# Instruction costs, diagonal scores and state order in a one-core decoder layer

## The chip, the core and the metric

One Trainium2 chip, one of its cores. The metric is the device time of one execution in microseconds (us): 1038.59 us is the median of three runs of the kernel before (1036.82 to 1039.56). A core has four compute engines that run side by side, each through its own queue in order: TensorE (PE) multiplies matrices, VectorE (DVE) and GpSimd (POOL) work elementwise, ScalarE (ACT) evaluates functions and casts. SyncE (SP) issues the large loads. An instruction starts when it is first in its queue and the semaphores that it waits for are there.

## The reference: one layer of a hybrid decoder

512 tokens of width 1024 pass through a mixing stage, a cross attention into 256 memory tokens, and a mixture of experts (32 experts). The change lies in the mixing stage. One input projection of the normalised tokens gives the columns of two branches and of their gates; the branches are projected back and merged:

```python
def conformer_conv_branch(a, gate, w_dw, b_dw, ln_g, ln_b, w_proj):
    u = a * jax.nn.sigmoid(gate)
    u = causal_depthwise_conv(u, w_dw, b_dw)          # 31 taps
    u = jax.nn.silu(layer_norm(u, ln_g, ln_b))
    return u @ w_proj
...
    def step(state, inp):                             # HGRN2, per chunk and head
        qb, kb, vb, fb = inp
        cum = jnp.cumsum(fb, axis=2)
        o_inter = jnp.einsum('bhtk,bhkv->bhtv', qb * jnp.exp(cum), state)
        ...
        scores = jnp.einsum('bhtk,bhtsk,bhsk->bhts', qb, decay, kb)
        o = o_inter + jnp.einsum('bhts,bhsv->bhtv', scores, vb)
        ...
```

Here `f` is the log of the forget gate, `k = 1 - f`, four heads of 128. The output of the recurrence is normalised per head, multiplied by `silu(g)` and projected by `hgrn_w_out`; the convolution's by `conv_w_out`. Each is multiplied by a sigmoid gate per channel (two gates of 1024 channels), the sum goes through `w_mix_out`.

## The kernel before: threads between the matmuls of the projections

**The projections.** `gemm_t` runs a projection with its output transposed (channels on partitions): 256 output columns at a time in two PSUM banks (`pt`), the contraction in chunks of 4 x 128. Inputs and weights are split into a high and a low part of type fp32r, and each product takes three matmuls of 128x512 (`hh` or `hl` by `wh` or `wl`); a chunk has 24 of them. A chunk's weights go a fixed way: SP loads `raw` (two buffers at this place), ACT casts it to `wh`, POOL subtracts to get `wl` in two pieces, TensorE multiplies. `ahead()` issues the splits three chunks ahead. The projections follow one another: V, f, q, u (the convolution's input, in four parts), g, the two gates (16 columns of 128, `ev_gate`), then `ev_rec` (from `oh`/`ol`, the recurrence's output split) and `ev_conv` (from `ch`/`cl`, the convolution's).

**The threads.** Between two matmul groups `pump()` steps generators: `hgrn_scores` (ending in `hgrn_state`), started before the q projection, and `conv`, started before u. A generator yields a time, and `pump` resumes it when the clock of the work issued has come to it. The clocks are kept by `Meter`: one for each of DVE, ACT, POOL and PE, which adds an estimated cost for every instruction at build time and holds the time at which each tile is ready. So the cost functions `dve_cost`, `act_cost`, `pool_cost` and `pe_cost` set the order of the program; on the chip the order is fixed.

**The recurrence.** `hgrn_scores` takes logarithms of `cum` (f) and `ck` (k) on ACT, four head pairs, then running sums along the tokens on DVE (`tensor_tensor_scan`, printed as SCALAR_TENSOR_TENSOR in the program order), and `ck = cum - ck`. Then for each of seven levels (blocks of 64, 32, ... 1 tokens) it makes a tile `z` (two subtractions on DVE, exp on ACT, one product with q on DVE), from which TensorE makes the scores of that level (`psc`), written into `ST` on ACT or DVE. The diagonal scores, `scores(7, kT, qT, ...)`, need only k and q: 16 matmuls in four banks, and four masked copies on DVE. `hgrn_state` goes through the four token blocks: outputs `po`, state updates `pst`, then a normalisation, and for each head four transposes of `oN` on TensorE (`pot`), a product into `gT` on DVE and the split `oh`/`ol`.

**The convolution.** 31 taps on DVE, for two channels blocks at a time, into PSUM banks (`cva`), reading `uT`. Then a layer norm over channels: column sums by eight matmuls of ones (`pmu`, and after the squares `pvar`), the root on DVE (`rsqrt_steps`), and for each of four blocks scaling on DVE, tanh on ACT, a product, and the split `ch`/`cl`.

**The buffers.** Tiles of 128x2048 (`unit`, `u4`) come from a ring of 16 buffers in the order in which the program asks for them; who asks gets the oldest buffer and waits until its last reader is done. Four gate tiles of four columns each are asked for in `ev_gate`, each at its first column.

Weights and threads aside, the experts' weights are loaded by SP from about 490 us on, and the stage behind 560 us is limited by these loads.

Of the kernel before, what the change touches and what calls it, by code (L numbers as in the profile page):

```python
# [42 lines left out]
class Meter:  # L43

    ready, port = {}, []

    def __init__(self, engine, cost):
        self.engine, self.cost, self.clock = engine, cost, 0.0  # L50
# [1 line left out]
    def __getattr__(self, name):  # L52
        f = getattr(self.engine, name)

        def call(*args, **kw):
            out = args[0] if args else kw["out"]
            aps = [a for a in list(args) + list(kw.values()) if hasattr(a, "tensor")]
            t = max([self.clock] + [Meter.ready.get(a.name, 0) for a in aps if a is not out])
            c = self.cost(out, kw)
            if name == "tensor_tensor" and c > 300 and all(a.space == SB for a in aps):  # L60

                for t0, t1, e in Meter.port[-4:]:
                    if e is not self and t0 <= t < t1:
                        t = t1
                Meter.port.append((t, t + c, self))
            self.clock = t + c
            for a in (out, kw.get("accum_out")):
                if a is not None:
                    Meter.ready[a.name] = self.clock + 60
            return f(*args, **kw)  # L70

        return call
# [28 lines left out]
def tile_layer(ctx, tc, x, mem, norm_mix_g, w_in, conv_w, conv_b, conv_ln_g, conv_ln_b, conv_w_out,  # L101
# [4 lines left out]
    nc = tc.nc  # L106
    meters = [Meter(e, c) for e, c in ((nc.vector, dve_cost), (nc.scalar, act_cost), (nc.gpsimd, pool_cost),
                                       (nc.tensor, pe_cost))]
    Meter.ready, Meter.port = {}, []
    V, S, G, PE = meters  # L110

    def dump(name, ap):
# [24 lines left out]
    def q4(name, dt=F32, tag="o"):  # L137
        return pool.tile([128, 1024], dt, name=name, tag=tag, bufs=BUFS[tag])

    def bank(name):  # L140
        return psum.tile([128, 512], F32, name=name, tag="b")
# [69 lines left out]
    done = set()  # L211

    def now():

        return max(m.clock for m in meters[:2])
# [409 lines left out]
    def hgrn_state():  # L625
        ST, qe, ke, elast = (state[n] for n in ("ST", "qe", "ke", "elast"))
        hs = q4("hs")[:, :512].rearrange("p (h v) -> p h v", h=4)
        oN = u4("oN")
        ssq, y, t = st[:, 16:32], st[:, 32:48], st[:, 48:64]
        sq = q4("sq")  # L630
        for b in range(NB):
            po = bank("po")
            for h in range(NH):
                sl = slice(h * 128, (h + 1) * 128)
                PE.matmul(po[:, sl], lhsT=ST[:, b, sl], rhs=Vn[b][:, sl], start=True, stop=b == 0)
                if b:
                    PE.matmul(po[:, sl], lhsT=qe[:, h, b * 128:(b + 1) * 128], rhs=hs[:, h, :],
                              start=False, stop=True)
            if b < NB - 1:
                pk = bank("pk")  # L640
                for h in range(NH):
                    PE.transpose(pk[:, h * 128:(h + 1) * 128], ke[:, h, b * 128:(b + 1) * 128], ident)
                kn = q4("kn")[:, :512]
                S.copy(out=kn, in_=pk)
                yield S.clock + 1500
                pst = bank("pst")
                for h in range(NH):
                    sl = slice(h * 128, (h + 1) * 128)
                    PE.matmul(pst[:, sl], lhsT=kn[:, sl], rhs=Vn[b][:, sl], start=True, stop=True)
                if b == 0:  # L650
                    S.copy(out=hs, in_=pst.rearrange("p (h v) -> p h v", h=4))
                else:
                    for h in range(NH):
                        V.scalar_tensor_tensor(hs[:, h, :], hs[:, h, :], elast[:, h * 4 + b:h * 4 + b + 1],
                                               pst[:, h * 128:(h + 1) * 128], op0=OP.mult, op1=OP.add)
            yield meters[3].clock + 1000
            S.copy(out=oN[:, b, :], in_=po)
            yield
            for h in range(NH):
                S.activation(sq[:, :128], oN[:, b, h * 128:(h + 1) * 128], AF.Square,  # L660
                             accum_out=ssq[:, b * 4 + h:b * 4 + h + 1])
            yield now()

        rsqrt(ssq, y, t, 4 * 128)
        V.tensor_scalar(y, y, 0.5, None, op0=OP.mult)
        for b in range(NB):
            ov = oN[:, b, :].rearrange("p (h v) -> p h v", h=4)
            V.tensor_tensor(out=ov, in0=ov, in1=y[:, b * 4:b * 4 + 4, None].to_broadcast([128, 4, 128]), op=OP.mult)
            yield
        yield now()  # L670
        yield from until("g")
        ohl.extend((u4("oh", F32R), u4("ol", F32R)))
        for h in range(NH):
            ps = bank("pot")
            for b in range(NB):
                PE.transpose(ps[:, b * 128:(b + 1) * 128], oN[:, b, h * 128:(h + 1) * 128], ident)
            V.scalar_tensor_tensor(gT[:, h, :], ps, vec("on", 0), gT[:, h, :], op0=OP.mult, op1=OP.mult)
            yield V.clock
            S.activation(ohl[0][:, h, :], gT[:, h, :], AF.Copy, scale=0.5)
            V.scalar_tensor_tensor(ohl[1][:, h, :], gT[:, h, :], 0.5, ohl[0][:, h, :].bitcast(F32),  # L680
                                   op0=OP.mult, op1=OP.subtract)
            yield V.clock

    def hgrn_scores():
# [62 lines left out]
        for li, m in enumerate(LEVELS):  # L747
            z = u4("z")
            zv, cv, qv, kv = (t.rearrange("p c (n two m) -> p (c n) two m", two=2, m=m) for t in (z, cum, qT, ck))
            mid = cv[:, :, 0, m - 1:m].to_broadcast([128, 1024 // m, m])  # L750
            V.tensor_tensor(out=zv[:, :, 0, :], in0=mid, in1=kv[:, :, 0, :], op=OP.subtract)
            V.tensor_tensor(out=zv[:, :, 1, :], in0=cv[:, :, 1, :], in1=mid, op=OP.subtract)
            yield V.clock
            S.activation(z, z, AF.Exp)
            ez = S.clock
            yield
            if prev is None:
                yield from until("q")
            else:
                yield from top_scores(prev, 2 * m, at) if li < 3 else scores(li - 1, prev, prev, at)  # L760
            yield ez
            V.tensor_tensor(out=zv[:, :, 1, :], in0=zv[:, :, 1, :], in1=qv[:, :, 1, :], op=OP.mult)
            at = V.clock + 2500
            yield
            prev = z
        yield from scores(7, kT, qT, 0)

        qe, ke = u4("qe"), u4("ke")
        state["qe"], state["ke"] = qe, ke
# [29 lines left out]
    def conv():  # L799
# [9 lines left out]
        for c2 in (0, 2):  # L809
# [12 lines left out]
            if c2 == 0:  # L822
                cv = u4("cv")
                chl.extend((u4("ch", F32R), u4("cl", F32R)))
            yield V.clock
            for c in (c2, c2 + 1):
                split(acc[c], c)
                S.copy(out=cv[:, c, :], in_=acc[c])
# [58 lines left out]
    def ev_gate(i, ps):  # L887
        w, i = i // 8, i % 8
        if i % 4 == 0:
            gates[w][i // 4] = u4("gate")  # L890
        S.activation(gates[w][i // 4][:, i % 4, :], ps, AF.Tanh, scale=0.5)

# [988 lines left out]
```

## Time and profile before

| | |
|---|---|
| median of three runs | 1038.59 us (1036.82 to 1039.56) |
| the profiled execution, its own time | 1040.21 us |
| its span in the profile | 1038.5 us |
| TensorE busy | 965.6 us, 93% |
| DVE, ACT, POOL busy | 479.6, 284.2, 255.5 us |
| mean granted clock of TensorE | 0.968 |

The profile gives one execution. The span is cut into stretches by the windows view: for each engine the busy time and the count of instructions, then the granted clock as a share of full speed. A timeline row is an instruction, or a run of the same, with its start and duration; the brackets give the idle time of the engine just ahead of it and what released it. The chain of waits is followed back from the last instruction of a stretch, and each piece is what the next one waited for. Matmuls are pipelined: one of 128x512 shows 0.39 us, but a row of them follows at a closer distance. All recorded instructions have line L70 before and L76 after, which is the line of the helper that records them.

### The profile page before, as it was taken

The numbers are of one execution on the slowest core, as the hardware profiler recorded it, in microseconds if no ns is written. First come the engines' busy times: TensorE is split into PE (matmuls) and PEld (weight loads), VectorE is DVE, ScalarE is ACT, GpSimd is POOL, SyncE is SP. The second block draws the span as 40 slices with busy tenths as digits, with TensorE's granted clock in tenths as the row PEclk, the third lists the DMA queues.
The fourth block names the chain that finished last, engine by engine and source line by source line (L and its number), as shares of the span: only waits on it lengthen the run. The fifth ranks groups of instructions, "written<-read, shape, count | busy, mean of one in ns | idle before, by whom it ended". The sixth has DMA issues, their size and how long they took to land.

```text
span 1038.5 us, 13293 instructions
## 1 busy us (share of the span) xinstructions
PE 965.6 (93%) x4951; PEld 630.0 (61%) x4951; DVE 479.6 (46%) x967; ACT 284.2 (27%) x467; POOL 255.5 (25%) x201
## 2 busy tenths in 40 slices
PE   7999989999999999999999999999879999687774
PEld 6888878888888788988874444444325544122221
DVE  6670567897976742545235233333203553010103
ACT  5633552335434333354411111011001110000003
POOL 2364642423445596341310000000000000000001
PEclk9999989999999999999999999999989999887988
DMA  9433221222323232224877999999999999999993
GB/s 339 170 88 102 82 64 58 62 82 68 96 63 100 89 116 88 73 83 171 344 282 293 382 373 418 417 418 415 420 417 419 418 418 416 419 418 419 415 391 139
DMA packets 80671, 260.81 MB, mean 251 GB/s; under 512 B 8475, under 2 KB 39356, under 8 KB 59996
## 3 DMA queue, kind: packets, MB, share of 16 engines
q1 hardware_dynamic: 75194, 252.81, 63.2%
q0 software_dynamic: 1728, 3.80, 1.0%
q10 hardware_dynamic: 3682, 3.32, 0.9%
q8 instruction: 40, 0.66, 0.3%
q14 instruction: 27, 0.22, 0.1%
HBM read 258.21 MB, written 4.19 MB: 253 GB/s over the span
## 4 chain that ended last, share of the span: by engine, by line
PE 69%; DMA 21%; DVE 5%; ACT 2%; SPq 2%; issue 1%; ACTq 0%; DVEq 0%
PE pt L70 24%; PE pg L70 12%; PE pn L70 12%; DMA wg<-in_moe_w_gate_dram 7%; DMA wd<-in_moe_w_down_dram 6%; PE py L70 5%; DMA wu<-in_moe_w_up_dram 5%; PE psc L70 3%; PE pc L70 3%; DMA raw<-in_xa_w_v_dram 2%; PE pd L70 2%; DVE z L70 1%; PE pot L70 1%; PE px L70 1%; PE pw L70 1%; DVE cum L70 1%
## 5 line engine op out<-in xcount | busy, mean ns | idle before, releaser
L70 POOL TENSOR_TENSOR wl<-raw,wh 128x512 fp32r<-128x512 f32 x158 | 219.1, 1409 | 288.3 <-ACT wh L70 288.0
L70 PE MATMUL py<-wd,sghd 128*32 128x512 f32 (+2 forms) x512 | 115.5, 645 | 18.8 <-DMA wd<-in_moe_w_down_dram 18.6
L70 ACT CAST wh<-raw 128x1024 fp32r<-128x1024 f32 x88 | 92.0, 1050 | 125.8 <-PE pt L70 75.3
L70 PE MATMUL pg<-wg,XT 128*32 128x512 f32 (+2 forms) x512 | 106.3, 624 | 12.4 <-DMA wg<-in_moe_w_gate_dram 12.2
L70 PE MATMUL pt<-hh,wh 128*128 128x512 f32 x288 | 115.0, 399 | 0.0
L70 PE MATMUL pt<-hh,wl 128*128 128x512 f32 x288 | 113.0, 392 | 0.0
L70 PE MATMUL pt<-hl,wh 128*128 128x512 f32 x288 | 112.9, 392 | 0.0
L70 PE MATMUL pg<-wu,XT 128*32 128x512 f32 (+2 forms) x512 | 104.8, 633 | 6.7 <-DMA wu<-in_moe_w_up_dram 6.6
L70 DVE TENSOR_TENSOR xs<-pc,xs 128x512 f32<-128x512 f32 x96 | 58.5, 680 | 89.4 <-PE pc L70 89.4
L70 POOL DMA_INDIRECT X<-xd,idx x12 | 12.1, 1008 | 343.9 <-DVE idx L70 174.8
L70 PEld LDWEIGHTS py<-wd,sghd 128*32 128x32 f32 (+2 forms) x512 | 31.8, 133 | 93.6 <-issue 54.4
L70 DVE SCALAR_TENSOR_TENSOR yl<-py,wsl,yh 128x512 fp32r<-128x512 f32 x26 | 19.4, 750 | 135.6 <-ACT yh L70 134.3
L70 PEld LDWEIGHTS pg<-wg,XT 128*32 128x32 f32 (+2 forms) x512 | 31.5, 132 | 82.7 <-issue 58.8
L70 DVE SCALAR_TENSOR_TENSOR cva<-uT,ca,cva 128x482 f32<-128x482 f32 (+29 forms) x120 | 78.6, 730 | 0.0
L70 PEld LDWEIGHTS pg<-wu,XT 128*32 128x32 f32 (+2 forms) x512 | 30.7, 132 | 73.1 <-issue 54.8
L70 PEld LDWEIGHTS pt<-hh,wl 128*128 128x128 f32 x288 | 54.5, 189 | 11.7
L70 PEld LDWEIGHTS pt<-hl,wh 128*128 128x128 f32 x288 | 54.7, 190 | 10.9
L70 PEld LDWEIGHTS pt<-hh,wh 128*128 128x128 f32 x288 | 54.7, 190 | 10.9
L70 ACT COPY sghd<-ph 128x512 f32<-128x512 f32 x13 | 7.6, 586 | 159.1 <-PE ph L70 159.1
L70 ACT ACTIVATE yh<-py,wsl 128x512 fp32r<-128x512 f32 x26 | 17.9, 688 | 116.8 <-PE py L70 116.5
L70 DVE SCALAR_TENSOR_TENSOR sghd<-pg,wsl,sghd 128x512 f32<-128x512 f32 x13 | 9.8, 751 | 84.3 <-PE pg L70 71.4
L70 PE MATMUL pt<-h,wh 128*128 128x512 f32 (+1 forms) x160 | 41.4, 348 | 0.0
(324 smaller groups left out, 1560.4 us busy)
## 6 DMA issues: line engine op xcount, KB each, us to landing
wg<-in_moe_w_gate_dram SPq DMA_DIRECT2D x57, 1024.0 KB
wd<-in_moe_w_down_dram SPq DMA_DIRECT2D x56, 1024.0 KB
wu<-in_moe_w_up_dram SPq DMA_DIRECT2D x52, 1024.0 KB
raw<-in_w_in_dram SPq DMA_DIRECT2D x40, 512.0 KB
wu<-in_moe_w_up_dram SPq DMA_DIRECT2D x24, 512.0 KB
wd<-in_moe_w_down_dram SPq DMA_DIRECT2D x16, 512.0 KB
wg<-in_moe_w_gate_dram SPq DMA_DIRECT2D x14, 512.0 KB
raw<-in_xa_w_v_dram SPq DMA_DIRECT2D x4, 1024.0 KB
```

The lines of the kernel that those rows point to most:

```text
L70: return f(*args, **kw)
```

## The change: costs of scans and table loads, order of diagonal, state and gate

The costs: a `tensor_tensor_scan` counts 1.75 times its former cost, and an activation that changes between Ln and any other function counts 1300 ns more on ACT's clock. In `hgrn_state` each block's output waits in the thread for a time `th` set from when the state tile is ready, and the thread marks `"st"` as done behind its loop over blocks. The diagonal scores move from behind the levels to the first level, right behind q. The convolution's split of its sums is stepped 1000 ns later. In `ev_gate`, a gate tile other than the first is asked for only when the recurrence's thread has been stepped through to `"st"`.

```diff
-    ready, port = {}, []
+    ready, port, log = {}, [], [False]
...
             c = self.cost(out, kw)
+            if name == "tensor_tensor_scan":
+                c *= 1.75
+            if name == "activation" and (args[2] == AF.Ln) != Meter.log[0]:
+
+                Meter.log[0] = not Meter.log[0]
+                c += 1300
...
-    Meter.ready, Meter.port = {}, []
+    Meter.ready, Meter.port, Meter.log = {}, [], [False]
...
         sq = q4("sq")
+        th = 0
         for b in range(NB):
+            yield th
             po = bank("po")
...
                                                pst[:, h * 128:(h + 1) * 128], op0=OP.mult, op1=OP.add)
+                th = Meter.ready[hs.name] + 500
             yield meters[3].clock + 1000
...
             yield now()
+        done.add("st")
...
             if prev is None:
                 yield from until("q")
+                yield from scores(7, kT, qT, V.clock + 1500)
             else:
...
             prev = z
-        yield from scores(7, kT, qT, 0)
...
                 chl.extend((u4("ch", F32R), u4("cl", F32R)))
-            yield V.clock
+            yield V.clock + 1000
...
         if i % 4 == 0:
+
+            while i + w and "st" not in done:
+                step(t_sc)
             gates[w][i // 4] = u4("gate")
```

The order of SP and of POOL stays as it was; that of ACT, DVE and TensorE differs between the f projection and the one from `ch`/`cl`. On TensorE, 216 split matmuls of the q projection and of u stand ahead of the first scores before (the first level's 16, then 21 split matmuls and the next level); after, 222 stand ahead of the diagonal's 16, and 24 more between these and the first level. Three other places are shown.

ACT, at the logarithms (`cum` and `ck` from f and k; `qT` is the q projection's tanh, `wh` the weight cast), before:

```order
L70 ACTIVATE cum<-cum 128x512
L70 ACTIVATE ck<-kT,tiny 128x512
L70 CAST wh<-raw 128x1024
L70 ACTIVATE cum<-cum 128x512
L70 ACTIVATE ck<-kT,tiny 128x512
L70 ACT_TABLE_LOAD
L70 ACTIVATE qT<-pt 128x512 x2
L70 CAST wh<-raw 128x1024 x2
```

and after:

```order
L76 ACTIVATE cum<-cum 128x512
L76 ACTIVATE ck<-kT,tiny 128x512
L76 ACT_TABLE_LOAD
L76 ACTIVATE qT<-pt 128x512
L76 ACT_TABLE_LOAD
L76 ACTIVATE cum<-cum 128x512
L76 ACTIVATE ck<-kT,tiny 128x512
L76 ACT_TABLE_LOAD
L76 ACTIVATE qT<-pt 128x512
L76 CAST wh<-raw 128x1024 x2
```

The first q column has moved in front of the last pair of logarithms, and there are two table loads more.

ACT, at the first column of the third gate tile (`gate`; buffer numbers tell the tiles apart: 2382 before and 2378 after are that tile, `oh` is the recurrence's output, `ch` and `cv` the convolution's), before:

```order
L70 ACTIVATE oh_2290<-gT_1671 128x512 [waits DVE_49]
L70 ACTIVATE gate_2382<-pt_2312 128x512 [waits DVE_49,PE_49]
L70 ACTIVATE gate_2382<-pt_2313 128x512 [waits PE_49]
L70 CAST wh_2413<-raw_2366 128x1024 [waits DMAHW2_49,Activation_49,Pool_49]
L70 ACTIVATE oh_2290<-gT_1671 128x512
L70 CAST wh_2450<-raw_2418 128x1024 [waits PE_49,DMAHW3_49,Activation_49,Pool_49]
L70 ACTIVATE gate_2382<-pt_2411 128x512 [waits PE_49]
L70 CAST ch_2001<-cva_2015 128x512
```

and after:

```order
L76 ACTIVATE gate_2378<-pt_2310 128x512 [waits PE_49]
L76 ACTIVATE gate_2378<-pt_2311 128x512
L76 CAST wh_2403<-raw_2362 128x1024 [waits DMAHW2_49,Activation_49,Pool_49]
L76 CAST wh_2444<-raw_2408 128x1024 [waits DMAHW3_49,Activation_49,Pool_49]
L76 ACTIVATE oh_2272<-gT_1667 128x512 [waits DVE_49]
L76 ACTIVATE gate_2378<-pt_2401 128x512
L76 ACTIVATE gate_2378<-pt_2402 128x512 [waits PE_49]
L76 CAST wh_2491<-raw_2449 128x1024 [waits DMAHW4_49,Activation_49,Pool_49]
L76 ACTIVATE oh_2272<-gT_1667 128x512 [waits DVE_49]
L76 CAST ch_2026<-cva_2055 128x512
```

The first eviction waited for DVE (the convolution's reads of `uT`) and TensorE before; after, it has the buffer of `oN`, and TensorE's transposes are what it waits for. One more `wh` cast stands ahead of `ch`.

TensorE, behind the column sums of the squares (`pvar`; `hh`, `hl` are the normalised tokens of the gate projection, `oh`, `ol` the recurrence's output of the next projection), before:

```order
L70 MATMUL pvar<-ch,onesr 128x512
L70 MATMUL pvar<-cl,onesr 128x512
L70 MATMUL pt<-hh,wh 128x512
L70 MATMUL pt<-hl,wh 128x512
L70 MATMUL pt<-hh,wl 128x512
```

and after:

```order
L76 MATMUL pt<-hh,wl 128x512
L76 MATMUL pt<-oh,wh 128x512
L76 MATMUL pt<-ol,wh 128x512
L76 MATMUL pt<-oh,wl 128x512
L76 MATMUL pvar<-ch,onesr 128x512
L76 MATMUL pvar<-cl,onesr 128x512
```

Before, 18 matmuls of the gate projection and 96 of the projection from `oh`/`ol` follow `pvar` up to the first that reads `ch`; after, 93 of the latter.

## Rows read from the trace of the kernel before

**Rows 1.** Busy time of each engine by stretch: us, instructions, granted clock, DMA share, GB/s

```profile
100.00:165.00 65.00, 60.65 (x346) 51.03 (x345) 35.86 (x29) 32.02 (x36) 31.18 (x19) 0.92 0.24 73
165.00:305.00 140.00, 140.00 (x745) 120.13 (x745) 121.98 (x184) 50.18 (x88) 49.94 (x38) 1.00 0.24 72
305.00:360.00 55.00, 54.04 (x237) 43.67 (x235) 38.45 (x49) 25.66 (x38) 30.07 (x22) 1.00 0.31 96
```

**Rows 2.** What TensorE waits for, 95 to 365 us: total us, times, longest

```profile
PE psc L70 <- DVE z L70: 4.4, 3, 2.2
```

**Rows 3.** Timeline of TensorE, 130 to 166 us: start, duration, what, count [idle before <- releaser]

```profile
135.31 2.05 PE L70 MATMUL psc<-z 128*64 128x64 f32 x32 [1.66 <-DVE z L70]
...
149.41 6.66 PE L70 MATMUL psc<-z 128*128 128x64 f32 x32 [2.17 <-DVE z L70]
...
156.82 0.63 PE L70 MATMUL pt<-hh,wl 128*128 128x512 f32 x1
157.25 0.63 PE L70 MATMUL pt<-hh,wh 128*128 128x512 f32 x1
```

**Rows 4.** Chain of waits, 100 to 215 us, in order of time: start, us, what

```profile
127.97 2.79 DVE z L70 x2
...
163.56 3.52 PE psc L70 x32
...
193.43 0.89 PE psc L70 x8
```

**Rows 5.** Busy time by stretch as in rows 1, one short stretch

```profile
150.00:160.00 10.00, 10.00 (x39) 9.13 (x39) 6.26 (x7) 2.61 (x2) 3.21 (x2) 0.50 0.20 60
```

**Rows 6.** Timeline of ACT, 104 to 147 us

```profile
114.22 0.71 ACT L70 ACTIVATE ck<-kT,tiny 128x512 f32<-128x512 f32 x1
114.95 1.28 ACT L70 ACT_TABLE_LOAD   x1
116.24 0.60 ACT L70 ACTIVATE qT<-pt 128x512 f32<-128x512 f32 x1
```

**Rows 7.** Timeline of DVE, 114 to 150 us

```profile
117.48 6.67 DVE L70 TENSOR_TENSOR_SCAN cum<-ca,cum 128x512 f32<-128x512 bf16 x4
```

**Rows 8.** Timeline of ACT, 286 to 330 us

```profile
302.31 1.09 ACT L70 ACTIVATE gate<-pt 128x512 f32<-128x512 f32 x2 [11.26 <-DVE cva L70]
...
312.70 1.05 ACT L70 CAST wh<-raw 128x1024 fp32r<-128x1024 f32 x1 [1.72 <-DMA raw<-in_w_in_dram]
...
326.37 1.05 ACT L70 CAST wh<-raw 128x1024 fp32r<-128x1024 f32 x1 [2.44 <-DMA raw<-in_hgrn_w_out_dram]
```

**Rows 9.** Chain of waits, 300 to 362 us

```profile
305.02 0.44 PE pot L70 x4
...
310.78 15.67 PE pt L70 x69
326.44 1.86 PE pvar L70 x8
...
357.36 0.70 DVE cl L70
...
358.10 3.93 PE pt L70 x16
```

**Rows 10.** Timeline of POOL, 284 to 330 us

```profile
304.41 5.50 POOL L70 TENSOR_TENSOR wl<-raw,wh 128x512 fp32r<-128x512 f32 x4 [11.26 <-ACT wh L70]
...
319.73 6.10 POOL L70 TENSOR_TENSOR wl<-raw,wh 128x512 fp32r<-128x512 f32 x4 [2.90 <-ACT wh L70]
```

**Rows 11.** Timeline of DVE, 326 to 362 us

```profile
344.83 1.37 DVE L70 TENSOR_TENSOR cl<-cv,ch 128x512 fp32r<-128x512 f32 x1 [0.68 <-ACT ch L70]
...
351.49 0.69 DVE L70 SCALAR_TENSOR_TENSOR gate<-gate,pt 128x512 f32<-128x512 f32 x1 [1.21 <-PE pt L70]
```

**Rows 12.** Timeline of TensorE, 766 to 778 us, in the expert stage

```profile
768.90 1.04 PE L70 MATMUL py<-wd,sghd 128*32 128x512 f32 x2 [2.22 <-DMA wd<-in_moe_w_down_dram]
```

**Rows 13.** Busy time by stretch as in rows 1, in the expert stage

```profile
771.00:778.00 7.00, 6.00 (x22) 1.15 (x26) 0.00 (x0) 0.00 (x0) 0.00 (x0) 0.51 1.02 414
```

## The prediction, made before the changed kernel ran

> **What bounds the kernel now.** I began with the busy time by stage [rows 1]. In 165:305 TensorE is busy without a break; in 100:165 it lacks 4.35 us of 65 and its granted clock is 0.92; in 305:360 it lacks 0.96 us. So in the part that the change touches TensorE sets the time, and time can be won only where it waits or runs slowly. The program order shows the same instructions on every engine from the w_mix projection (about 362 us) on; what is won or lost before 362 us therefore reaches the expert stage unchanged, where the loads follow the frees of TensorE's buffers. I take it one to one to the end.
>
> The second view is what TensorE waits for in 95:365: nearly everything is psc on DVE's z, 4.4 us in three waits, the longest 2.2 [rows 2]. The timeline of TensorE [rows 3] puts them at 135.3 (1.66 us) and 149.4 (2.17 us), with a short one between; the reader is to see that the score matmuls at 149.41 take 6.66 us, whereas the same 32 take 3.52 us at 163.56 [rows 4], and that the split matmuls behind them stand 0.43 us apart [rows 3] instead of the 0.227 that I work out below. The granted clock of 150:160 is 0.50 [rows 5]: right after the third wait TensorE drops to the lower level, 1.2 GHz, for 10 us.
>
> **Early part: what goes.** The waits for z come from a late chain on ACT and DVE. With the diagonal scores moved ahead, TensorE has 16 score matmuls and 24 split matmuls in front of the first level. Walk of the new order: ACT's last logarithm ended at 114.93 [rows 6]; without the fourth pair (about 1.2 us) it comes to the load at 113.7. Then load (1.28), qT (0.60), load, the fourth pair, load, qT: 120.0. DVE multiplies that qT (0.7) and starts its four scans at 120.7 instead of 117.48 [rows 7]; ck, the third q column and the two halves of z stand behind them as before and end 3.2 us later, the second half at 134.0 instead of 127.97 + 2.79 = 130.8 [rows 4]. The last q column (0.6) is there at 134.6. TensorE has done 222 split matmuls instead of 216 by then: before, the 216 ended at 133.5 (135.31 less the wait of 1.66, [rows 3], rounded for the tail of a matmul), so 6 more end at 134.9. The diagonal's four banks take 4 x 0.89 [rows 4] to 138.4. DVE's copies and z times q end near 140.5. TensorE's 24 split matmuls end at 143.85, so the first level has 3.3 us of cover; the following levels have, by the same count, 2.3, 1.2 and 4.0 us. The narrow place is the diagonal itself, with 0.3 us. I cost it at nothing; if it is missed it costs what it is missed by.
>
> Gain: the three waits, 4.4 us [rows 2], and the lower clock: 6.66 - 3.52 = 3.1 for the scores and nine split matmuls at 0.43 - 0.227, 1.8. Together **-9.3 us**. Ends: -4.4 if a new wait makes the clock fall once more there, -9.3 if none does.
>
> **The two additional table loads** lie in that walk at 1.28 us each. Before, the load starts 0.02 us after the last logarithm ends, and qT starts 0.01 us after the load ends [rows 6], so a switch costs its load and nothing around it.
> The Trainium skill, "ScalarE: Activation LUTs", section "What ACT_TABLE_LOAD costs", adds a pipeline drain of about 1.4 us to a load of about 1.3. By that the two extra switches would come to 5.3 us, an estimate from that page, and the sum would be 2.5 us worse at the diagonal; the rows of this trace show the load and not the drain.
>
> **Middle: the gate tile behind the state.** Before, ACT stood 11.26 us at the first column of the third gate tile for the convolution, whose input tile had the buffer [rows 8]. Now that tile takes the buffer of oN, which the fourth group of head transposes reads last. In the new order TensorE has 54 split matmuls (0.227 each: 15.67 us for 69) and two groups of transposes (0.44 each, [rows 9]) between that column's last matmul and the end of that group: 13.1 us in which ACT stands, with two gate evictions, two wh casts and the rest queued behind it, POOL's wl behind the casts, and raw's loads on SP behind wl. The weights split ahead last for 60 split matmuls, so 6 (1.4 us) are left when ACT is released. ACT then needs 0.6 + 0.5 + 1.05 (gates x2 and wh, [rows 8]) = 2.1: TensorE waits 0.8. The first wl comes 1.4 us later [rows 10], two matmuls (0.45) cover part: 0.9 more. Then the loads: before, the next wh but one came 10.4 us after ACT's release because its raw had just landed [rows 8]; the convolution's ch and cl were cast in front of it, now they stand behind it. raw can be loaded when wl has read the buffer, 4.9 us after release, and lands 3.6 to 5.5 us after that: a wh waits for it until 326.37 and 312.70 [rows 8], and the first half of POOL's four wl ahead of each ended at 322.8 and 307.2 [rows 10]. With 3.6: wh ends at 9.6 us after release, then oh 0.6 and two rounds of ch, cl, cv at about 1.9, that is 14 us less what pmu's first matmuls can do while the last halves are made (some 1.9): about 12 against the 9.9 (36 x 0.227 + 1.7) at which TensorE comes to pmu. I take 2.3, **+4.0 us** for the middle. Bounds: 0 if the casts are as little in the way as before, when the stall of 11.26 us cost TensorE nothing, and 6 with the landing of 5.5.
>
> **Tail: the variance.** From the end of pvar to the last cl there is a chain on DVE and ACT: 326.44 + 1.86 to 357.36 + 0.70 is 29.8 us [rows 9], of it 0.68 idle in DVE ahead of each of two cl and 1.21 ahead of a gate [rows 11]. TensorE has 114 split matmuls behind pvar before the first that reads ch, and ten more to the first that needs the last cl: 124 x 0.227 = 28.1, so 1.6 us are late; they stand as waits and a broken pipeline just ahead of 358.10 [rows 9]. In the new order pvar stands 21 split matmuls later: 93 + 10 = 103, 23.4 us. Two of the gate multiplications come into the reciprocal root and fewer stand between the last casts, so the chain is between 27.2 (no idle) and 29.8; I take 28.5. Late by 5.1 instead of 1.6: **+3.5 us** (1.9 to 4.8).
>
> **The clock behind it.** Waits of 5.1 us in all within some 7 us are more than those that the clock followed at 149.4. In the expert stage, a wait of 2.22 us at 768.90 [rows 12] is followed by 771:778 at a clock of 0.51 [rows 13]. So I expect the lower level again, behind 350 us, for 3.4 to 10.2 us (the lengths seen in this trace); at half the speed 1.7 to 5.1 us. I take 6.8 us: **+3.4**. Nothing if the waits are spread thinly.
>
> **Sum.** -9.3 + 4.0 + 3.5 + 3.4 = +1.6 us. The profiled execution took 1040.21 us, 1.6 us above the median of 1038.59; in its terms 1041.8, against the median **1040.2 us**.
>
> **Rivals.**
> 1. *Faster.* The clock holds behind 350 us and the middle costs TensorE little. For it: a stall of ACT of 11.26 us was free before [rows 8]. Sum: -9.3 + 0 to 2 + 3.5 = -5.8 to -3.8, 1032.8 to 1034.8; with the middle at 4.0 and the clock at its full level it is -1.8, 1036.8, which is no measurable change. Chance of beyond -3.1: 0.25.
> 2. *Slower*, by one mechanism: raw lands late behind ACT's stand at oN. SP's load waits for wl, wl for wh, wh for the gate eviction, and ch and cl for wh in one queue. From a landing of 5.1 us after wl on (the sum is then +3.1) it is slower; at 5.5, with pmu waiting 4.2 us, the clock falls there as well, for 6.8 us: -9.3 + 6 + 3.5 + 3.4 + 3.4 = +7.0, 1045.6; without that fall 1042.2. Chance of beyond +3.1: 0.27, in which I count case 3.
> 3. *It does not do what it says*: the diagonal, with 0.3 us of cover, waits for the last q column, and the clock falls early as it did. A wait of 2.2 us at the diagonal and 4.9 of lower clock come back: 1040.2 + 7.1 = 1047.3. Chance 0.06.
> 4. *The extra loads cost more than their rows*: if each of the two holds ACT for as long again as the load itself (1.28), the diagonal waits 2.6 - 0.3 = 2.3 us: 1042.5. The rows around the load leave no room for it [rows 6]; chance 0.03, in the 0.27 as well.
> This is the case that the Trainium skill's page "ScalarE: Activation LUTs", under the section cited, would make with its drain.
>
> **How the numbers follow.** A measurement here tells some 0.3%, 3.1 us, from no change. The forecast and its neighbours within 3.1 us (rival 1 with a full middle among them) have 0.48. The range leaves out the thicker ends of both sides: low 1033.5 (rival 1 with 1 us for the middle), high 1045.5 (rival 2).
>
> **What would show it.** The waits of psc for z gone, no slice at half clock in 145:165, four table loads on ACT by 120 us instead of two: early part right. ACT's gate waiting some 13 us for TensorE's transposes instead of 11.3 for the convolution; TensorE's waits for wh and wl near 1.7 us and for pmu near 2.3: middle right. TensorE's waits for cl and ch near 350 us about 5 us in all and a clock of 0.5 behind them: tail right. If 305:360 holds under 2 us of idle, the middle and tail are wrong and the kernel is faster; if psc waits for qT, the early part is.

## The result, and the profile after

The changed kernel takes 1044.7 us (median of six runs, 1042.68 to 1045.82), the kernel before 1037.8 us in its six (1036.62 to 1039.56). The ratio is 1.0064 with an interval of 1.0048 to 1.0080: 5 to 8.3 us slower. The forecast was 1040.2 us and no measurable change, the range 1033.5 to 1045.5. The time lies in the range, near its end; the likeliest case is not the one that came, which is the slower one.

The busy time of after by stretch, columns as in [rows 1]:

```profile
100.00:165.00 65.00, 63.57 (x389) 53.75 (x388) 41.23 (x35) 33.91 (x38) 31.99 (x21) 1.00 0.26 81
165.00:305.00 140.00, 137.31 (x722) 116.79 (x721) 120.87 (x179) 52.91 (x89) 55.23 (x39) 1.00 0.23 71
305.00:360.00 55.00, 49.07 (x201) 37.92 (x199) 36.48 (x47) 22.98 (x35) 23.17 (x17) 0.97 0.28 89
```

In 100:165 TensorE lacks 1.43 us instead of 4.35, and its granted clock is 1.00 instead of 0.92. In 165:305, without a break before, it lacks 2.7 us, and in 305:360 5.9 instead of 0.96. What TensorE waits for in after, 95 to 380 us (total, times, longest), in place of [rows 2]:

```profile
PE pt L76 <- ACT ch L76: 2.7, 3, 1.7
PE psc L76 <- DVE qT L76: 1.4, 1, 1.4
PE pmu L76 <- ACT ch L76: 1.4, 2, 0.8
PE pot L76 <- DVE oN L76: 1.3, 1, 1.3
PE pmu L76 <- DVE cl L76: 1.0, 1, 1.0
PE pt L76 <- DVE cl L76: 0.9, 2, 0.6
PE pt L76 <- ACT wh L76: 0.7, 1, 0.7
PE pt L76 <- POOL wl L76: 0.6, 1, 0.6
```

psc no longer waits for z, but 1.4 us for qT; in all 10 us of waits are spread over four places (q at 136 us, oN at 272, wh to pmu at 300 to 312, ch and cl at 354 to 360). At the last two of them the granted clock falls, as the windows view shows for two short stretches:

```profile
312.00:315.00 3.00, 2.69 (x6) 1.87 (x7) 0.69 (x1) 2.24 (x4) 0.38 (x1) 0.51 0.53 175
...
360.00:363.00 3.00, 2.97 (x6) 2.11 (x7) 1.64 (x3) 0.92 (x1) 2.00 (x2) 0.50 0.00 0
```

Two marks bound the part that the change touches: the last transpose of the first norm (56.94 us before, 55.65 after) and the first matmul of w_mix (377.73 and 381.54). Between them lie 320.8 us before and 325.9 after, +5.1; this part is called "the stretch" below. From w_mix to the first expert matmul both take 184.5 us. In these two executions the stretch begins 1.3 us earlier after than before and the expert stage is 1.3 us shorter, so the profiled executions (1042.68 us, the fastest of the six of after, and 1040.21 us before) are 2.5 us apart. The medians are 6.9 us apart, 1.8 us more than the two stretches; the interval covers 5.1 and 6.9.

### The profile page after: what moved, and what is told of

Same layout as the page of the kernel before. It is cut to its first block, busy times and chain, and to the rows that moved or that the text cites. A ratio compares the mean times of both kernels' runs of the same rounds, so it can differ in the third digit from the quotient of the medians.

```text
span 1040.9 us, 13288 instructions
## 1 busy us (share of the span) xinstructions
PE 960.3 (92%) x4951; PEld 628.1 (60%) x4951; DVE 483.6 (46%) x967; ACT 287.5 (28%) x469; POOL 256.5 (25%) x201
## 4 chain that ended last, share of the span: by engine, by line
PE 63%; DMA 24%; DVE 7%; ACT 3%; issue 2%; POOL 0%; SPq 0%; ACTq 0%; POOLq 0%; DVEq 0%
PE pt L76 21%; PE pn L76 12%; PE pg L76 11%; DMA wd<-in_moe_w_down_dram 8%; DMA wg<-in_moe_w_gate_dram 7%; DMA wu<-in_moe_w_up_dram 7%; PE py L76 5%; PE psc L76 3%; PE pc L76 3%; DVE cva L76 2%; PE pd L76 1%; PE pot L76 1%; PE px L76 1%; DVE st L76 1%; PE pw L76 1%
## 5 line engine op out<-in xcount | busy, mean ns | idle before, releaser
L76 PE MATMUL py<-wd,sghd 128*32 128x512 f32 (+2 forms) x512 | 109.0, 623 | 19.0 <-DMA wd<-in_moe_w_down_dram 18.7
L76 PE MATMUL pg<-wg,XT 128*32 128x512 f32 (+2 forms) x512 | 105.6, 622 | 14.4 <-DMA wg<-in_moe_w_gate_dram 14.3
```

## Experiments

Twelve kernels, each with its own runs of the kernel before beside it; the ratios go by these runs. The waits are the gaps between TensorE's matmuls, in us, in four parts of the stretch: up to the first head transposes (early), up to pmu (heads), up to pvar (pmu), up to w_mix (tail). The last column is the time at the lower clock level (1.2 GHz) inside the stretch. The stretch, the waits and the low clock come from one profiled execution of each kernel, the median from all of its runs.

| kernel | median us | ratio to before, 95% | stretch | early | heads | pmu | tail | low clock |
|---|---|---|---|---|---|---|---|---|
| before | 1037.8 | | 320.8 | 4.4 | 0 | 0 | 1.0 | 10.2 |
| after | 1044.7 | 1.0064 (1.0048 to 1.0080) | 325.9 | 1.4 | 2.7 | 2.4 | 3.6 | 3.4 + 3.4 |
| 1 diagonal alone | 1035.2 | 0.9980 (0.9966 to 0.9994) | 317.3 | 1.7 | 0 | 0 | 2.2 | 6.8 |
| 2 after, no table cost | 1035.9 | 0.9991 (0.9977 to 1.0005) | 318.6 | 1.7 | 0 | 0 | 2.9 | 6.8 |
| 3 after, pvar early | 1040.6 | 1.0041 (1.0024 to 1.0058) | 323.9 | 1.4 | 2.7 | 2.3 | 1.7 | 6.8 |
| 4 diagonal, pvar early | 1028.8 | 0.9927 (0.9905 to 0.9949) | 311.2 | 1.7 | 0 | 0 | 0 | 0 |
| 5 after, heads early | 1038.2 | 0.9998 (0.9986 to 1.0011) | 320.4 | 1.4 | 1.3 | 0 | 3.4 | 6.8 |
| 6 kernel 4, heads late | 1033.1 | 0.9957 (0.9942 to 0.9971) | 314.2 | 1.7 | 0 | 1.9 | 0 | 0 |
| 7 table cost alone | 1045.5 | 1.0083 (1.0063 to 1.0104) | 326.9 | 4.0 | 0.7 | 2.8 | 2.2 | 3.4 + 6.8 |
| 8 diagonal later, heads and pvar early | 1028.6 | 0.9914 (0.9892 to 0.9937) | 309.8 | 0.3 | 0 | 0 | 0 | 0 |
| 9 after without three parts | 1048.1 | 1.0107 (1.0068 to 1.0146) | 328.4 | 2.4 | 2.7 | 2.7 | 2.9 | 3.4 + 6.8 |
| 10 scan cost alone | 1040.5 | 1.0030 (1.0013 to 1.0046) | 323.6 | 1.2 | 2.0 | 4.4 | 1.0 | 6.8 |
| 11 convolution later alone | 1050.5 | 1.0126 (1.0086 to 1.0166) | 332.1 | 4.4 | 1.9 | 2.8 | 2.9 | 10.2 + 3.4 + 3.4 |
| 12 after, convolution not later | 1042.0 | 1.0048 (1.0031 to 1.0064) | 325.7 | 1.4 | 0.7 | 3.4 | 2.2 | 6.8 + 6.8 |

The median follows the stretch within 2 us (+11.4 in the stretch of kernel 11 and +11.7 in its time, -9.6 and -9.0 in kernel 4, -6.6 and -5.4 in kernel 6). And the stretch follows the columns: kernel 8 has a single wait of 0.3 us at 309.8, so 309.5 without it; the waits and half of the low clock added to that give 319.9 for before, 323 for after and 316.8 for kernel 1. The rest goes with the number of waits: 0.8 us with 6 of them before, 2.9 with 12 after, 0.6 with 3 in kernel 1. The first matmul after a wait takes 0.50 instead of 0.39 us, and the next starts late.

**1, the diagonal alone** (on before).

```diff
                 yield from until("q")
+                yield from scores(7, kT, qT, V.clock + 1500)
...
-        yield from scores(7, kT, qT, 0)
```

> The kernel before with one part of the change alone: the diagonal scores first. Its order has the two table loads of before, the third gate tile in oN's buffer but with the last head transposes 61 instead of 40 matmuls ahead of pmu, and 105 split matmuls between pvar and the first that reads ch (before 114, after 93). Theory (the early gain is real; the loss comes from ACT's stand at the gate tile and from pvar's late place): the waits for z and the low clock at 150:160 are gone, one wait of about 1.2 us for q's last column; no wait in 165:310; about 3 us more of waits near 350 than before and perhaps a short clock fall there. From the last transpose of the norm to the first w_mix matmul 317 us (before 320.8, after 325.9), time about 1034. Rival (the diagonal's early place itself loses, since it makes TensorE wait for q and leaves less to do later): 322 or more, time 1039 or more.

Stretch 317.3, time 1035.2: the theory's numbers, the rival's are excluded. What TensorE waits for, same view as above:

```profile
PE psc L75 <- DVE qT L75: 1.7, 1, 1.7
PE pt L75 <- ACT ch L75: 1.5, 1, 1.5
PE pt L75 <- DVE cl L75: 0.6, 1, 0.6
```

z is gone from it. The wait for q is 1.7 us with only the two table loads of before, but it ends another chain than in after. Here ACT has the exponential of z in front of the last q column, and DVE stands 1.87 us for that column:

```profile
130.84 1.92 ACT L75 ACTIVATE z<-z 128x2048 f32<-128x2048 f32 x1 [4.66 <-DVE z L75]
...
133.27 0.69 DVE L75 SCALAR_TENSOR_TENSOR qT<-qT,pt 128x512 f32<-128x512 f32 x1 [1.87 <-ACT qT L75]
```

In after ACT has that column ready at 127.55, and DVE comes to it late, behind the scans and z. So the wait doesn't need the additional loads, but this kernel does not show what they do to it in after.

**2, after without the table cost.**

```diff
-                c += 1300
```

> The changed kernel without the 1300 ns for a change between Ln and other functions: two table loads as before instead of four, scores early, pvar at the place of after (93). The last head transposes stand 67 matmuls ahead of pmu instead of 40. Theory: the middle's loss (about 8 us with its clock fall) goes nearly whole, because the stand of ACT at the third gate tile gets shorter; the tail's loss (4.7) stays. The stretch 320.5, time about 1038. Rival (the table loads cost nothing but their 2.6 us; the middle's loss comes from the convolution's later split alone, which this kernel keeps): stretch 323 or more, waits for pmu as in after, time 1041 or more.

Stretch 318.6, time 1035.9, better than the theory's number: heads and pmu have no wait at all. The tail has 2.9 us of waits (3.6 in after) and the clock falls behind it. The rival falls: the convolution's later split is in this kernel and costs the middle nothing.

**3, after with pvar early.**

```diff
-        yield V.clock + 500
+        yield V.clock + (-3000)
         pvar = col_sum(chl, "pvar")
```

> The changed kernel with the thread's wait ahead of pvar shortened, so that 108 split matmuls instead of 93 follow pvar; all else as in after. Theory of the prediction (the tail's loss is the number of matmuls between pvar and ch): the waits near 350 fall from 3.6 to about 1, the clock stays up behind them, stretch 325.9 - 3.4 - 1.7 = 321, time about 1040. Rival (pvar then waits itself for the squares' low parts, since these are late already; the wait only moves): a wait of some 3 us ahead of pvar, stretch 325, time about 1044.

Stretch 323.9, time 1040.6, between the theory's numbers and the rival's. The waits of the tail view:

```profile
PE pt L76 <- ACT ch L76: 0.5, 1, 0.5
PE pvar L76 <- ACT ch L76: 0.5, 1, 0.5
PE pt L76 <- DVE cl L76: 0.5, 2, 0.2
PE pvar L76 <- DVE cl L76: 0.2, 1, 0.2
```

ch and cl behind pvar cost 1.0 instead of 3.6 us, as the theory has it; pvar itself waits 0.7, which is the rival's in kind and not in size. The low clock behind the tail is gone, but the one in the middle lasts 6.8 instead of 3.4 us.

**4, diagonal and pvar early** (the two edits of 1 and 3 on before, with -2000).

> The kernel before with the diagonal scores first and pvar's wait shortened: 117 split matmuls between pvar and ch, two table loads. Theory: early gain as in the first kernel, no wait in the middle, under 2 us of waits near 350 and no clock fall: stretch 313, time about 1030. Rival (waits ahead of pvar or the expert stage's loads take the gain): stretch 313 but time within 3 us of before, or stretch 317.

Stretch 311.2, time 1028.8, where the theory had 313 and 1030. One wait is left:

```profile
PE psc L75 <- DVE qT L75: 1.7, 1, 1.7
```

Its third gate tile has oN's buffer, as in after. ACT's timeline there:

```profile
290.61 1.09 ACT L75 ACTIVATE gate<-pt 128x512 f32<-128x512 f32 x2 [8.36 <-PE pot L75]
...
299.40 1.05 ACT L75 CAST wh<-raw 128x1024 fp32r<-128x1024 f32 x1 [0.67 <-DMA raw<-in_w_in_dram]
```

ACT stands 8.36 us for the transposes and 0.67 for the raw behind it, and TensorE does not notice.

**5, after with the heads early.**

```diff
-            yield V.clock
+            yield V.clock - 2000
             S.activation(ohl[0][:, h, :], gT[:, h, :], AF.Copy, scale=0.5)
...
-            yield V.clock
+            yield V.clock - 2000
```

> The changed kernel with the thread's two waits in the loop over heads 2000 ns shorter, so that the last of the four groups of head transposes stands 67 matmuls ahead of pmu instead of 40; scores, table loads and pvar's place (90) as in after. Theory (the middle's loss is the stand of ACT at the third gate tile, whose buffer those transposes read, and the late raw behind it): ACT's stand falls from 14.4 to 8 us, no wait of TensorE in 290:315 and no clock fall there, tail as in after: stretch from the norm's last transpose to w_mix 319.8 (after 325.9), time about 1038.5. Rival (the middle's loss comes from the convolution's cast standing behind wh, whatever ACT stands at): stretch 324 or more, time 1043 or more.

Stretch 320.4, time 1038.2, at the theory's numbers. What ACT waits for, 200 to 345 us:

```profile
ACT gate L76 <- PE pot L76: 9.5, 1, 9.5
...
ACT wh L76 <- DMA raw<-in_w_in_dram: 1.3, 1, 1.3
```

ACT stands 9.5 instead of 14.4 us, and its wait for raw is 1.3 instead of 5.2; pmu waits for nothing and the clock holds there. The 1.3 us left in "heads" are the first transposes waiting for oN.

**6, kernel 4 with the heads late**: the second of these two waits is `V.clock + 1500`.

> The kernel with the diagonal first and pvar early, with the same two waits lengthened (the first unchanged, the second by 1500 ns): the last transposes stand 49 matmuls ahead of pmu instead of 61, nothing else of its early part or of pvar's place (117) changes. Theory: ACT's stand grows from 8.4 by some 3 to 5 us, raw lands later, pmu waits about 3 us, and the clock falls there: stretch 311.2 + 3 + 1.7 = 316, time about 1033.5. Rival (a longer stand is covered by the weights split ahead): stretch 311 to 312, time 1029.

Stretch 314.2, time 1033.1. ACT stands 11.53 us, and pmu waits:

```profile
294.72 1.09 ACT L75 ACTIVATE gate<-pt 128x512 f32<-128x512 f32 x2 [11.53 <-PE pot L75]
...
302.97 0.63 ACT L75 ACTIVATE oh<-gT 128x512 fp32r<-128x512 f32 x1 [4.26 <-DVE gT L75]
...
306.12 0.58 ACT L75 CAST ch<-cva 128x512 fp32r<-128x512 f32 x1
```

```profile
PE pmu L75 <- ACT ch L75: 1.5, 2, 0.9
PE pmu L75 <- DVE cl L75: 0.5, 2, 0.2
```

The theory's direction, with 1.9 instead of 3 us, and without the clock fall that I had added; +3.0 in the stretch for +3.2 in the stand. With 5, a later or earlier place of the transposes, and with it a longer or shorter stand, makes and unmakes the middle's loss. Raw's landing is not what makes it here: between the release and ch, ACT waits 4.26 us for gT, which is made from the last transposes, and 1.07 for raw (0.67 in kernel 4).

**7, the table cost alone** (the Ln lines of the change on before).

> The kernel before with the 1300 ns for table changes alone: four table loads, diagonal scores where they were, last transposes 40 matmuls ahead of pmu, 105 behind pvar. Theory: the first level's wait for z goes (it comes behind more matmuls), two of about 1 us stay, the clock may hold; the middle and the tail lose as in after: stretch 323 to 325 (before 320.8), time 1041 or so. Rival (the table cost is what makes the early gain): stretch 317 or less, time 1035.

Stretch 326.9, time 1045.5: worse than the theory, far from the rival. The middle and tail lose as in after. Of the early gain only the clock is there, which holds; 4.0 us of waits for z stay. TensorE's first two waits for z and the windows row behind the third (0.72 us):

```profile
138.92 2.08 PE L76 MATMUL psc<-z 128*64 128x64 f32 x32 [1.99 <-DVE z L76]
...
146.56 2.11 PE L76 MATMUL psc<-z 128*32 128x32 f32 x64 [1.25 <-DVE z L76]
```

```profile
148.00:160.00 12.00, 11.28 (x84) 9.69 (x81) 9.06 (x8) 5.81 (x5) 5.68 (x4) 1.00 0.14 45
```

**8, all early**: kernel 4 with the diagonal at `V.clock + 3000` and the heads' second wait at `V.clock - 3000`.

> The kernel before with the diagonal first but 1500 ns later on the thread's clock (so that q's last column is there), the heads' second wait 3000 ns shorter (last transposes 76 ahead of pmu) and pvar early (117 behind it). Theory: the wait of 1.7 us for q that the fourth kernel has goes as well: stretch 311.2 - 1.3 = 309.9, time about 1027.5. Rival (this wait comes back at z, since the levels start later): stretch 311 or more, time 1029 or more.

Stretch 309.8, as the theory; 1028.6 us, of the 1.4 us less in the stretch only 0.2 shows in the time, within its interval. TensorE's idle time from 100 to 360 us, columns as in [rows 1], is 0.3 us in all:

```profile
100.00:165.00 65.00, 64.68 (x411) 55.28 (x410) 40.83 (x38) 33.24 (x37) 31.80 (x21) 1.00 0.26 81
165.00:305.00 140.00, 140.00 (x721) 119.19 (x720) 120.58 (x181) 56.66 (x96) 54.59 (x41) 1.00 0.25 76
305.00:360.00 55.00, 55.00 (x244) 45.51 (x243) 40.79 (x52) 23.52 (x35) 33.14 (x23) 1.00 0.30 96
```

It beats before and after: 0.9914 of before (0.9892 to 0.9937).

**9, after without three of its parts**: the loop in `ev_gate`, the times `th`, the factor on the scans.

> The changed kernel without three of its parts: the wait for the state in ev_gate, the times th in hgrn_state, and the factor on the scans. Without the first two the program's order is that of after, word for word; without the third the diagonal's scores stand three split matmuls earlier and one q column elsewhere. Theory (diagonal, table cost and the convolution's 1000 ns make the whole result): stretch within 1 us of 325.9, time about 1044. Rival (the scan factor has an effect of its own): 3 us from it or more.

Stretch 328.4, time 1048.1. Its order differs from that of after in two places: the diagonal stands three split matmuls earlier, and one q column's product on DVE has moved. That is the factor's doing; the first two parts change no instruction's place in this kernel. Without the factor the wait for q is 2.4 instead of 1.4 us, and the low clock behind the tail 6.8 instead of 3.4 us. By the stretch the factor gains 2.5 us, short of the rival's 3 and more than the theory's 1; by the medians, which are 3.4 us apart, it reaches the rival's 3. The longer low clock stands behind 2.9 us of waits in the tail, fewer than the 3.6 in after; that the factor made it longer is not shown.

**10, the scan cost alone** (on before).

> The kernel before with the factor 1.75 on scans alone: two table loads, diagonal late, last transposes only 19 matmuls ahead of pmu, 111 behind pvar. Theory: early about 2 us of wait for z instead of 4.4; the stand of ACT at the gate tile is long and pmu late: waits of 5 to 8 us in 290:315 and a clock fall, the tail about as before: stretch 326 to 328, time about 1044. Rival (with pvar at its place of before nothing is lost): stretch under 320, time 1037.

Stretch 323.6, time 1040.5. The middle is as the theory has it, with 6.4 us of waits and ACT standing 16.1 us. The stretch is 2.4 us under the theory's lower end: early there is a single wait of 1.2 us, where I had put about 2, and no low clock.

**11, the convolution later alone** (`yield V.clock + 1000` on before).

> The kernel before with the convolution's split stepped 1000 ns later, alone: early part as before (three waits for z, the low clock), last transposes 37 matmuls ahead of pmu, 105 behind pvar. Theory: the early part's 10 us stay, the middle loses some 6 to 8 us with its clock fall, the tail 2 to 4: stretch 330, time about 1048. Rival (the later split costs nothing while TensorE has other work): stretch 321 to 323, time 1039.

Stretch 332.1, time 1050.5: the theory, and 2 us more. The early waits and the low clock are those of before, and ACT stands 15.4 us at the gate tile, for the transposes: 1000 ns on a build-time clock cost 11.7 us.

**12, after with the convolution not later.**

> The changed kernel without the convolution's additional 1000 ns: four table loads, last transposes 40 matmuls ahead of pmu as in after, 105 instead of 93 matmuls behind pvar. Theory (ACT's stand at the third gate tile follows from the place of the transposes, the tail from the place of pvar): middle as in after (ACT's stand 13 to 15 us, pmu waits 2 to 3, clock falls), tail 1.5 us better: stretch 324 to 325, time about 1043. Rival (the later split is what loses the middle here too, as it did alone): stretch 318 or less, time 1037.

Stretch 325.7, time 1042.0. ACT stands 13.8 us, the middle loses 4.1 us of waits as in after (5.1), the tail 2.2 instead of 3.6 and the clock falls for longer. It is the theory's case, 0.7 us over its upper end; the rival's 318 is excluded. So the step that costs 11.4 us of the stretch on before costs 0.2 us of it in after: what one of these costs does depends on the others.

## Why the prediction was right or wrong, step by step

**Bound and carrying over: right.** The stretch decides, and from w_mix to the first expert matmul the time is the same to 0.01 us.

**Early part: right in what goes, wrong at the diagonal; -9.3 was -7.9.** The first head transposes stand 224.0 us behind the first mark before and 214.1 after, with nine split matmuls (2.0 us) fewer ahead of them. The waits for z and the 10 us at 1.2 GHz are gone. The step that failed is "the narrow place is the diagonal itself, with 0.3 us. I cost it at nothing"; the prediction's own sign of a wrong early part, psc waiting for qT, came. The diagonal waits 1.43 us, and some 0.3 more goes with the restart. The walk used the durations of before; in after DVE's four scans take 7.72 instead of 6.67 us [rows 7] and z's second half 2.30 instead of 1.22, together 2.1 of the 2.5 us by which q's last column is later than in the walk. That column follows z on DVE without a break:

```profile
119.74 7.72 DVE L76 TENSOR_TENSOR_SCAN cum<-ca,cum 128x512 f32<-128x512 bf16 x4
...
132.86 2.30 DVE L76 TENSOR_TENSOR z<-cum 128x1024 f32<-128x1024 f32 x1
135.09 0.67 DVE L76 SCALAR_TENSOR_TENSOR qT<-qT,pt 128x512 f32<-128x512 f32 x1
```

POOL's wl run beside them:

```profile
120.12 8.43 POOL L76 TENSOR_TENSOR wl<-raw,wh 128x512 fp32r<-128x512 f32 x4 [5.92 <-ACT wh L76]
```

Before, POOL runs beside the scans for 4.4 of their 6.67 us, and it stands idle from 128.5 to 134.2, where z's second half takes 1.22 (1.21 in kernel 1, with POOL idle as well); after, it runs for 7.3 of the scans' 7.72 us and for the first 1.2 us of that half. So both are longer where POOL runs beside them longer; no run moves POOL's work alone.

**Table loads: right.** ACT's timeline in after, in place of [rows 6]:

```profile
112.75 1.28 ACT L76 ACT_TABLE_LOAD   x1
114.04 0.60 ACT L76 ACTIVATE qT<-pt 128x512 f32<-128x512 f32 x1
114.66 1.28 ACT L76 ACT_TABLE_LOAD   x1
115.95 0.63 ACT L76 ACTIVATE cum<-cum 128x512 f32<-128x512 f32 x1
```

A load, qT 0.01 us behind it, and the next load 0.02 us behind qT's end: two additional switches cost 2.6 us of ACT and nothing around them. Rival 4, in which each holds ACT for as long again, is excluded by these rows. The drain of some 1.4 us that the Trainium skill, "ScalarE: Activation LUTs", section "What ACT_TABLE_LOAD costs", adds does not appear in these rows.

**Middle: the chain was the right one, the sum was too small (+4.0 predicted, +8.3 measured).** From the first head transposes to pvar the changed kernel takes 15.1 us more, with 30 split matmuls (6.8 us) more between them. ACT's timeline, in place of [rows 8]:

```profile
297.90 1.09 ACT L76 ACTIVATE gate<-pt 128x512 f32<-128x512 f32 x2 [14.40 <-PE pot L76]
...
307.61 1.05 ACT L76 CAST wh<-raw 128x1024 fp32r<-128x1024 f32 x1 [5.23 <-DMA raw<-in_w_in_dram]
...
309.09 0.57 ACT L76 CAST ch<-cva 128x512 fp32r<-128x512 f32 x1
```

The stand is 14.40 us for the transposes (13.1 predicted) instead of 11.26 for the convolution. TensorE's waits in that place:

```profile
271.60 0.33 PE L76 MATMUL pot<-ident,oN 128*128 128x128 f32 x1 [1.34 <-DVE oN L76]
...
299.98 0.50 PE L76 MATMUL pt<-hh,wh 128*128 128x512 f32 x1 [0.71 <-ACT wh L76]
...
301.33 0.50 PE L76 MATMUL pt<-hh,wl 128*128 128x512 f32 x1 [0.63 <-POOL wl L76]
...
309.71 0.49 PE L76 MATMUL pmu<-ch,onesr 128*128 128x512 f32 x1 [0.80 <-ACT ch L76]
311.20 0.50 PE L76 MATMUL pmu<-cl,onesr 128*128 128x512 f32 x1 [1.00 <-DVE cl L76]
312.31 0.80 PE L76 MATMUL pmu<-ch,onesr 128*128 128x512 f32 x1 [0.60 <-ACT ch L76]
```

wh and wl 1.34 us in all (1.7 predicted), pmu 2.4 (2.3 predicted). So the prediction's signs for the middle came, and its sum still was half of what was measured. Two terms were missing, put at nothing. The first transposes wait 1.34 us for oN on DVE; I had not thought of a wait there. And at 312, within the third of pmu's waits, the lower clock comes for 3.4 us (1.7 us lost), which the prediction had only in its second rival. The rest, some 1.5 us, goes with the restarts behind six waits. The second rival came in part: raw landed 4.96 us after wl, in the chain of waits of after,

```profile
300.01 2.53 POOL wl L76 x2
...
302.55 4.96 DMA raw<-in_w_in_dram
...
330.35 1.86 PE pvar L76 x8
...
358.03 0.69 DVE cl L76
```

against 3.6 in the likeliest case and 5.1 from which on the rival was to decide. The clock fell as in the rival, but with 2.4 us of waits for pmu and not with 4.2, and for 3.4 us, not 6.8. Its time with that fall was 1045.6 and 1044.7 was measured; they lie this near in part by luck, since the rival had neither the wait for q nor the one for oN. The runs on the stand are 5 and 6: it is made shorter in after and longer in kernel 4, with the diagonal where it was and pvar within three matmuls of its place. That raw is what holds ch in after is read from the rows above, where ACT stands 5.23 us for it; no run moves raw alone.

What I put wrongly in words is whose doing the stand is. Neither the loop in `ev_gate` nor `th` moves anything; the third gate tile has oN's buffer in kernels 1, 2, 4 and 8 as well, where the stand is covered. What moves the last transposes nearer to pmu is the costs on the build-time clocks: after without the table cost has them 67 matmuls ahead, with it 40. The stand of 11.26 us before cost nothing while one of 11.53 us in kernel 6 did. The rows show a difference in ACT's queue: before, the first ch of this place started 3.9 us after the release at 302.31,

```profile
306.18 0.60 ACT L70 CAST ch<-cva 128x512 fp32r<-128x512 f32 x1
```

2.6 us before TensorE came to pmu (308.75); in kernel 6 it started 11.4 us after the release, 1.3 us after TensorE had come there (304.78). The buffers, the place of the transposes and that of ch and cl differ together, and no run separates them.

**Tail: right in place and sign; +3.5 was +2.6, and the clock's +3.4 was 1.7 in this execution.** With the restarts the tail lost 4.7 us where 6.9 were predicted. pvar ends at 332.21 and the last cl at 358.72: 26.5 us (28.5 taken, 27.2 the lower end); why the chain is shorter still I did not trace. TensorE waits 3.57 us instead of 0.96, where about 5 were predicted. By the prediction's own numbers the lower end of its term is +2.2 and not +1.9 (27.2 - 23.4 - 1.6). The low clock behind it lasts 3.4 us in after and in kernel 11, 6.8 in kernels 1, 2, 5, 7, 9 and 12. Kernels 3 and 4 show that pvar's place is the cause.

**Chances.** The sum -9.3 + 4.0 + 3.5 + 3.4 = +1.6 was in truth -7.9 + 8.3 + 4.7 = +5.1. Early part and middle were 5.7 us worse than predicted and the tail with its clock 2.2 better; that the time lies in the range owes something to that. The middle's own bounds (0 to 6) held its waits for wh, wl and pmu, and neither its clock fall nor the wait for oN. A wait that is priced at nothing with 0.3 us of cover should have carried half of its miss, and a chain of waits that I expected to total 4 us in the middle should have carried the clock's price, as I did in the tail.

## What to carry to other kernels

Where a planner's build-time costs set the order, a more exact cost is one more perturbation: each of three corrections (table change, scan, convolution's step) alone made this kernel slower, by 7, 2 and 12 us, and the one edit that took work off a known wait (the diagonal) made it faster. Their effects do not add up: the convolution's step costs 11.4 us of the stretch on before and 0.2 in after (kernels 11 and 12). Look first at which wait ends last, move that work by hand, then place the next ones (heads, pvar) by the count of matmuls between a producer and its reader; three hand-placed steps gave 0.9914, of which the heads' step and the later diagonal add nothing clear of noise to the 0.9927 of kernel 4. A buffer given to an eviction on ACT is paid by everything queued behind it: here stands of 8.4 and 9.5 us for the transposes cost TensorE nothing behind them, one of 11.5 us did.

## What the hardware showed that I had not expected

Waits of 1.66, 0.52 and 2.17 us (before) were followed by the lower clock for 10.2 us, and so were the same waits in kernel 11. Waits of 1.99, 1.25 and 0.72 us, ahead of the same scores but with other numbers of split matmuls between (kernel 7), were not: the granted clock of 148:160 is 1.00 there. In after the lower clock came for 3.4 us within the third of three waits for pmu, 2.4 us in all; four waits of 1.9 us in all at the same place (kernel 6) brought none; in the tail of kernel 1 it came for 6.8 us within the second of two waits, 2.2 us in all. At half the speed, some 2 us of waits thus cost 2 us, or 4 to 6. Each kernel has one trace, and the mean granted clock of one kernel's executions differs (0.966 to 0.983 in the 28 of before that stand beside kernels 1 to 4, the expert stage included); whether the same waits are followed by the same fall each time is not shown.
